# Loading the second piece of x over the scalar queue, ahead of the parameters

## The chip, the cores and the metric

The kernel runs on one core of one Trainium2 chip. The metric is the device time of one execution in microseconds (us); lower is better. Loads are DMA transfers from HBM to SBUF, stores go the other way. HBM is the memory of the chip, SBUF that of the core, with 128 partitions. Two queues are used: the sync queue (q1 in the profile, issued by SP) and the scalar queue (q10, issued by ACT). Both are worked off by the same 16 DMA engines. ACT is the engine that runs the ACTIVATE instructions (func(x * scale + bias)); PE multiplies matrices, DVE and POOL do the small rest, and SP only issues transfers here. A q behind an engine's name (ACTq, SPq) marks what its issuing part does.

## The reference

Batch normalisation with fixed statistics, then ReLU, on 16.8 MB of float32:

```python
def reference(x, gamma, beta, running_mean, running_var, eps):   # x: 32 x 128 x 32 x 32
    normalized = (x - running_mean[None, :, None, None]) / np.sqrt(running_var[None, :, None, None] + eps)
    scaled = normalized * gamma[None, :, None, None] + beta[None, :, None, None]
    return np.maximum(scaled, 0)
```

Per channel this is relu(x * scale + bias), so the kernel reads 16.8 MB, does one ACTIVATE per 128 x 1024 elements, and writes 16.8 MB.

## The kernel before

x is seen as 2 halves (t) of 128 partitions with 16 rows of 1024 numbers each (4 KB a row). It is loaded in six pieces; I call them x0, x2, x4, x8 (rows 0 to 2, 2 to 4, 4 to 8, 8 to 16 of the first half) and y0, y8 (rows 0 to 8 and 8 to 16 of the second).

```python
PIECES = (((0, 2), (2, 4), (4, 8), (8, 16)), ((0, 8), (8, 16)))
STORE_CUTS = {(0, 1)}
...
for t in range(T):
    for a, b in PIECES[t]:
        xt = data.tile([P, b - a, HW], F32, name=f"x{t}_{a}")
        nc.sync.dma_start(out=xt, in_=xr[t, :, a:b, :])
        tiles.append((t, a, b, xt))
raw = params.tile([Q, 4, J], F32, name="raw")
for k, src in enumerate((running_var, gamma, running_mean, beta)):
    nc.scalar.dma_start(out=raw[:, k, :], in_=src.rearrange("(q j) -> q j", j=J))
# ... cut: a matmul spreads the parameters, then sqrt, reciprocal, three products -> scale_t, bias_t
for t, a, b, xt in tiles:
    first = a
    for j in range(a, b):
        nc.scalar.activation(out=xt[:, j - a, :], in_=xt[:, j - a, :], func=ACTF.Relu,
                             bias=bias_t[:, j : j + 1], scale=scale_t[:, j : j + 1])
        if j + 1 == b or (t, j + 1) in STORE_CUTS:
            nc.scalar.dma_start(out=outr[t, :, first : j + 1, :], in_=xt[:, first - a : j + 1 - a, :])
            first = j + 1
```

A piece of n rows is one contiguous run of n x 4 KB on each partition. In the packet records a piece is 128 packets, one for each partition, that is 8 for each of 16 DMA engines: of 8 KB for x0, of 32 KB for x8, and so on. The first store is cut in two with 4 KB packets, those of x2, x4 and x8 have 8, 16 and 32 KB.

Of the kernel before, what the change touches and what calls it, by code (L numbers as in the profile page):

```python
# [1 line left out]

# [4 lines left out]


F32 = mybir.dt.float32
ACTF = mybir.ActivationFunctionType  # L10



J = 16

PIECES = (((0, 2), (2, 4), (4, 8), (8, 16)), ((0, 8), (8, 16)))

STORE_CUTS = {(0, 1)}


@with_exitstack
def kernel(
    ctx: ExitStack,
    tc: tile.TileContext,
    x: bass.AP,
    gamma: bass.AP,
    beta: bass.AP,
    running_mean: bass.AP,
    running_var: bass.AP,
    eps: bass.AP,  # L30
    out: bass.AP,
):
    nc = tc.nc
    B, C, H, W = x.shape
    HW = H * W
    P = nc.NUM_PARTITIONS
    assert C % J == 0 and P % (C // J) == 0 and (B * C) % (P * J) == 0
    Q = C // J
    T = B * C // (P * J)

    xr = x.rearrange("b c h w -> (b c) (h w)").rearrange("(t p j) w -> t p j w", p=P, j=J)
    outr = out.rearrange("b c h w -> (b c) (h w)").rearrange("(t p j) w -> t p j w", p=P, j=J)

    data = ctx.enter_context(tc.tile_pool(name="data", bufs=1))
    params = ctx.enter_context(tc.tile_pool(name="params", bufs=1))
    psum = ctx.enter_context(tc.tile_pool(name="psum", bufs=1, space=bass.MemoryType.PSUM))

    tiles = []
    for t in range(T):
        for a, b in PIECES[t]:  # L50
            xt = data.tile([P, b - a, HW], F32, name=f"x{t}_{a}")
            nc.sync.dma_start(out=xt, in_=xr[t, :, a:b, :])  # L52
            tiles.append((t, a, b, xt))


# [4 lines that stand above are left out]
    eps_t = params.tile([P, 1], F32, name="eps_t")  # L60
    nc.vector.memset(eps_t, float(eps))  # L61
    rep = params.tile([Q, P // Q, Q], F32, name="rep")
    nc.gpsimd.memset(rep, 1.0)  # L63
    nc.gpsimd.affine_select(  # L64
        out=rep,
        in_=rep,
        compare_op=mybir.AluOpType.is_equal,
        fill=0.0,
        base=0,
        pattern=[[0, P // Q], [-1, Q]],  # L70
        channel_multiplier=1,
    )
    cols = psum.tile([P, 4, J], F32, name="cols")
    nc.tensor.matmul(  # L74
        cols.rearrange("p k j -> p (k j)"),
        rep.rearrange("q r s -> q (r s)"),
        raw.rearrange("q k j -> q (k j)"),
        start=True,
        stop=True,
    )  # L80
    std_t = params.tile([P, J], F32, name="std_t")
    nc.scalar.activation(out=std_t, in_=cols[:, 0, :], func=ACTF.Sqrt, bias=eps_t[:, 0:1], scale=1.0)  # L82
    rstd_t = params.tile([P, J], F32, name="rstd_t")
    nc.vector.reciprocal(out=rstd_t, in_=std_t)  # L84
    scale_t = params.tile([P, J], F32, name="scale_t")
    nc.vector.tensor_mul(out=scale_t, in0=cols[:, 1, :], in1=rstd_t)  # L86
    ms_t = params.tile([P, J], F32, name="ms_t")
    nc.vector.tensor_mul(out=ms_t, in0=cols[:, 2, :], in1=scale_t)  # L88
    bias_t = params.tile([P, J], F32, name="bias_t")
    nc.vector.tensor_sub(out=bias_t, in0=cols[:, 3, :], in1=ms_t)  # L90

    with tc.manual_schedule(engines={mybir.EngineType.Activation}):
# [3 lines that stand above are left out]
                nc.scalar.activation(  # L96
                    out=xt[:, j - a, :],
                    in_=xt[:, j - a, :],
                    func=ACTF.Relu,
                    bias=bias_t[:, j : j + 1],  # L100
                    scale=scale_t[:, j : j + 1],
                )
                if j + 1 == b or (t, j + 1) in STORE_CUTS:
                    nc.scalar.dma_start(
                        out=outr[t, :, first : j + 1, :], in_=xt[:, first - a : j + 1 - a, :]
                    )
                    first = j + 1


# [1 line left out]
_INS = ['x', 'gamma', 'beta', 'running_mean', 'running_var', 'eps']  # L111
_OUTS = [((32, 128, 32, 32), 'float32')]

_NUMBERS = {'eps': 1e-05}


# [26 lines left out]
```

## Time and profile before

| | before |
|---|---|
| time, median of 3 runs | 83.86 us (83.7 to 83.93) |
| span in the profile | 81.9 us |
| packet time, both queues (96.2% of the span) | 78.8 us |
| ACT busy | 38.5 us |
| first ACTIVATE on x | 9.72 us |
| loads end, last store ends | 46.1 us, 80.6 us |

A queue row of the profile gives packets, megabytes, and the time of these packets as a share of 16 engines' span. Share times span is the time for which the average engine worked for this queue. A row of the windows gives from:to and length, busy time of PE, PEld, DVE, ACT and POOL, the clock of TensorE, the DMA share and GB/s. A packet counts where it starts, so a short window can show a share over 1.

### The profile page before, as it was taken

How to read it: one execution, taken by the hardware profiler on the slowest of the kernel's cores; microseconds unless marked ns; L12 is line 12 of the kernel's file. 1: busy time of each engine (PE TensorE's matmuls, PEld its weight loads, DVE VectorE, ACT ScalarE, POOL GpSimd, SP SyncE). 2: the span in 40 equal slices, each digit the busy share in tenths (PEclk: the TensorE clock that was granted, in tenths of full speed). 3: DMA queues.
4: the chain of work that ended last, by engine and by line, in shares of the span. 5: the costliest groups of instructions: out<-in, count | busy, mean ns of one | idle time of the engine just before them, and what ended most of it. 6: DMA issues, size and time to landing. Idle time of an engine off the chain costs nothing.

```text
span 81.9 us, 119 instructions
## 1 busy us (share of the span) xinstructions
PE 0.7 (1%) x2; PEld 0.5 (1%) x2; DVE 0.8 (1%) x5; ACT 38.5 (47%) x34; POOL 0.8 (1%) x6
## 2 busy tenths in 40 slices
PE   0002000000000000000000000000000000000000
PEld 0002000000000000000000000000000000000000
DVE  0000300000000000000000000000000000000000
ACT  0600377799039999199994199993000000000000
POOL 3000000000000000000000000000000000000000
DMA  2899999989899999979789798996999899799690
GB/s 32 328 425 472 408 448 448 512 352 494 370 448 416 446 418 396 500 296 600 320 380 580 304 464 384 512 512 288 480 512 400 368 512 448 320 512 496 272 512 0
DMA packets 1936, 33.56 MB, mean 410 GB/s; under 512 B 272, under 2 KB 272, under 8 KB 528
## 3 DMA queue, kind: packets, MB, share of 16 engines
q1 hardware_dynamic: 864, 16.78, 48.4%
q10 hardware_dynamic: 1072, 16.78, 47.8%
HBM read 16.78 MB, written 16.78 MB: 410 GB/s over the span
## 4 chain that ended last, share of the span: by engine, by line
DMA 56%; ACT 11%; SPq 0%; issue 0%
DMA x<-in_x_dram 56%; ACT x L96 11%; SPq L52 0%
## 5 line engine op out<-in xcount | busy, mean ns | idle before, releaser
L96 ACT ACTIVATE x<-x,bias_t,scale_t 128x1024 f32<-128x1024 f32 x32 | 37.0, 1228 | 10.3 <-DMA x<-in_x_dram 7.9
L82 ACT ACT_TABLE_LOAD x1 | 1.3, 1283 | 2.6 <-issue 2.6
L82 ACT ACTIVATE std_t<-cols,eps_t 128x16 f32<-128x16 f32 x1 | 0.3, 273 | 4.5 <-PE cols L74 4.5
L74 PE MATMUL cols<-raw,rep 8*128 8x64 f32 x2 | 0.7, 428 | 7.7 <-DMA raw<-in_beta_dram 7.7
L74 PEld LDWEIGHTS cols<-raw,rep 8*128 8x128 f32 x2 | 0.5, 304 | 7.7 <-issue 7.7
L64 POOL TENSOR_SCALAR_AFFINE_SELECT rep<-rep 8x128 f32<-8x128 f32 x1 | 0.4, 392 | 0.1
L84 DVE RECIPROCAL rstd_t<-std_t 128x16 f32<-128x16 f32 x1 | 0.3, 254 | 7.8 <-ACT std_t L82 7.8
L63 POOL MEMSET rep<- 8x128 f32 x1 | 0.2, 195 | 0.3 <-POOLq L124 0.3
L86 DVE TENSOR_TENSOR scale_t<-cols,rstd_t 128x16 f32<-128x16 f32 x1 | 0.2, 175 | 0.1
L90 DVE TENSOR_TENSOR bias_t<-cols,ms_t 128x16 f32<-128x16 f32 x1 | 0.2, 175 | 0.0
L88 DVE TENSOR_TENSOR ms_t<-cols,scale_t 128x16 f32<-128x16 f32 x1 | 0.2, 175 | 0.0
L124 POOL MEMSET const-bfloat16-1.0<- 128x1 bf16 x1 | 0.1, 106 | 0.0
L124 POOL MEMSET const-uint8-127<- 128x1 uint8 x1 | 0.1, 106 | 0.0
L124 POOL MEMSET const-float32-0.0<- 128x1 f32 x1 | 0.1, 103 | 0.3 <-issue 0.3
L124 POOL MEMSET const-float32-1.0<- 128x1 f32 x1 | 0.1, 103 | 0.0
L61 DVE MEMSET eps_t<- 128x1 f32 x1 | 0.1, 59 | 0.9 <-PEq L124 0.9
## 6 DMA issues: line engine op xcount, KB each, us to landing
x<-in_x_dram SPq DMA_DIRECT2D x3, 4096.0 KB, 38.8
out_dram<-x ACTq DMA_DIRECT2D x3, 4096.0 KB, 27.9
x<-in_x_dram SPq DMA_DIRECT2D x2, 1024.0 KB, 5.7
x<-in_x_dram SPq DMA_DIRECT2D x1, 2048.0 KB, 11.2
out_dram<-x ACTq DMA_DIRECT2D x1, 2048.0 KB
out_dram<-x ACTq DMA_DIRECT2D x2, 512.0 KB, 18.8
out_dram<-x ACTq DMA_DIRECT2D x1, 1024.0 KB
raw<-in_running_var_dram ACTq DMA_DIRECT2D x1, 0.5 KB
```

The source lines that it names most:

```text
L61: nc.vector.memset(eps_t, float(eps))
L63: nc.gpsimd.memset(rep, 1.0)
L64: nc.gpsimd.affine_select(out=rep, in_=rep, compare_op=mybir.AluOpType.is_equal, fill=0.0, base=0, pattern=[[0, P // Q], [-1, Q]], channel ...
L74: nc.tensor.matmul(cols.rearrange("p k j -> p (k j)"), rep.rearrange("q r s -> q (r s)"), raw.rearrange("q k j -> q (k j)"), start=True, s ...
L82: nc.scalar.activation(out=std_t, in_=cols[:, 0, :], func=ACTF.Sqrt, bias=eps_t[:, 0:1], scale=1.0)
L84: nc.vector.reciprocal(out=rstd_t, in_=std_t)
L86: nc.vector.tensor_mul(out=scale_t, in0=cols[:, 1, :], in1=rstd_t)
L88: nc.vector.tensor_mul(out=ms_t, in0=cols[:, 2, :], in1=scale_t)
L90: nc.vector.tensor_sub(out=bias_t, in0=cols[:, 3, :], in1=ms_t)
L96: nc.scalar.activation(out=xt[:, j - a, :], in_=xt[:, j - a, :], func=ACTF.Relu, bias=bias_t[:, j : j + 1], scale=scale_t[:, j : j + 1],)
L124: nc = _bacc.Bacc("TRN2", target_bir_lowering=False, num_devices=1)
```

## The change

The second piece, x2, is issued by ACT and not by SP, in front of the parameters. The intent is to have two pieces under way at once from the start.

```diff
+PIECES_SCALAR = (0, 2)
 ...
-            nc.sync.dma_start(out=xt, in_=xr[t, :, a:b, :])
+            eng = nc.scalar if (t, a) == PIECES_SCALAR else nc.sync
+            eng.dma_start(out=xt, in_=xr[t, :, a:b, :])
```

## The prediction

> **What bounds the kernel now.** I read the page first, then the chain of waits, the waits themselves, the windows and the timeline. The page's strip of DMA business and its queue rows:
>
> ```profile
> DMA  2899999989899999979789798996999899799690
> ...
> q1 hardware_dynamic: 864, 16.78, 48.4%
> q10 hardware_dynamic: 1072, 16.78, 47.8%
> HBM read 16.78 MB, written 16.78 MB: 410 GB/s over the span
> ```
>
> q1 is the sync queue (864 packets, all loads of x), q10 the scalar queue (four parameters and all stores). 48.4 + 47.8 = 96.2% of the span of 81.9 us, that is 78.8 us, is time in which the DMA engines work on a packet. That leaves 3.1 us. The windows say where it lies and how fast the rest runs (last columns: TensorE clock, DMA share, GB/s):
>
> ```profile
> 0.00:1.50 1.50, 0.00 (x0) 0.00 (x0) 0.06 (x1) 0.00 (x0) 0.80 (x6) 1.00 0.00 0
> 1.50:2.50 1.00, 0.00 (x0) 0.00 (x0) 0.00 (x0) 0.00 (x0) 0.00 (x0) 1.00 0.70 123
> 3.00:8.00 5.00, 0.27 (x2) 0.30 (x2) 0.00 (x0) 0.90 (x1) 0.00 (x0) 1.00 1.02 430
> 20.00:46.00 26.00, 0.00 (x0) 0.00 (x0) 0.00 (x0) 18.85 (x17) 0.00 (x0) 1.00 1.00 428
> 46.00:80.00 34.00, 0.00 (x0) 0.00 (x0) 0.00 (x0) 9.16 (x8) 0.00 (x0) 1.00 1.01 436
> 80.00:81.90 1.90, 0.00 (x0) 0.00 (x0) 0.00 (x0) 0.00 (x0) 0.00 (x0) 1.00 0.00 0
> ```
>
> There are 1.5 us before the first byte, about 1.5 us after the last one, and between them no hole: 430 GB/s with loads alone, 428 with loads and stores mixed, 436 with stores alone. So this is a copy of 33.56 MB at one rate. The chain names the load of x (56%) and the last eight ACTIVATEs (11%), and stops at 55.95 us:
>
> ```profile
> 7.99 38.77 DMA x<-in_x_dram
> 46.76 0.03 issue
> 46.79 9.16 ACT x L96 x8
> ```
>
> The chain follows waits between instructions, and nothing after 55.95 us waits except the program's end. The last store is issued at 55.97 us. The stores then take until 80.3 us, so at 434 GB/s 24.3 us x 434 = 10.5 MB were still to be written. The last store is 4.2 MB, that is 9.7 us. It could have come as late as 80.3 - 9.7 = 70.6 us without leaving the DMA engines a gap. **ACT has about 14.6 us of slack at the end**, and its idle time does not set the span.
>
> **What the Trainium skill says.** (1) "DMA: Bandwidth & Descriptors", section "Issuing engines are not separate DMA queues": transfers from sync and scalar run on the same 16 engines and interleave, and issuing from two engines saves only sequencer time. The trace agrees: the two queues together give 428 GB/s, one alone 430. (2) The same page, "Where 436 GB/s comes from", gives a ceiling of 435.2 GB/s; 428 to 436 here is that ceiling. (3) The same page, "Queues, rings and completion order": each DMA engine takes turns between the queues it has work for, packet by packet. The trace agrees in kind: in the mixed stage one load packet of 32 KB (1.213 us in the packet records) alternates with one store packet (0.159 us for 4 KB). (4) The same page, "Latency and other measured facts", gives about 600 ns to a first byte on these queues; here the first issue starts at 0.81 us and the first packet at about 1.5, so 0.7 us.
>
> **The change, part by part.**
>
> Removed from sync: the second issue (x rows 2 to 4, 1 MB). The issue took about 0.43 us, from 1.23 to 1.66 us. The issues of x4 and x8 move up by about that. Worth nothing by itself: the first piece keeps the engines in work for 1 MB / 430 GB/s = 2.4 us from 1.57 us on, and the second was in the queue by then.
>
> Added to scalar: the same issue in front of the four parameter issues, which begin now at 0.81 us:
>
> ```profile
> 0.81 7.51 SPq L52 DMA_DIRECT2D x<-in_x_dram  x6
> 0.81 0.59 ACTq L59 DMA_DIRECT2D raw<-in_running_var_dram  x1
> 1.43 0.29 ACTq L59 DMA_DIRECT2D raw<-in_gamma_dram  x1
> 1.75 0.31 ACTq L59 DMA_DIRECT2D raw<-in_running_mean_dram  x1
> 2.08 0.45 ACTq L59 DMA_DIRECT2D raw<-in_beta_dram  x1
> 7.73 0.65 PE L74 MATMUL cols<-raw,rep 8*128 8x64 f32 x2 [7.73 <-DMA raw<-in_beta_dram]
> ...
> 9.72 1.24 ACT L96 ACTIVATE x<-x,bias_t,scale_t 128x1024 f32<-128x1024 f32 x1 [1.03 <-DVE bias_t L90]
> ```
>
> The issues of the parameters start some 0.4 to 0.6 us later. The possible gain is in the ramp: from 1.5 to 2.5 us only 123 GB/s move, (430 - 123) / 430 = 0.7 us of lost transfer. The first packet of each engine takes up to 1.0 us where the later ones of 8 KB take 0.309. Two queues that open at once may cover part of that first wait. I allow **0 to 0.3 us, 0.1 expected**.
>
> The cost is in the order of the packets. Each engine holds 8 packets of x0 and 8 of x2. Before they came one after the other on one queue, x0 first. Now they take turns, so both end near 1.57 + 0.5 (first packet) + 16 x 0.309 = 7.0 us, landing at about 7.3 us. x0 landed at about 5.2 us before; x2 hardly moves. The parameters now stand behind x2 in the scalar queue. In the packet records of before, the later three went between load packets of 8 KB, data and completion write each taking a turn (0.31 us apart). After the change they meet the 16 KB packets of x4 (0.611 us): four data packets and four completion writes are eight turns, so about 7.0 + 7 x 0.61 = 11.3 us, with landing and semaphore 11.8 to 12.3 us, against 7.7 before. From the matmul to the first ACTIVATE it is 9.72 - 7.73 = 2.0 us, so **the first ACTIVATE moves from 9.72 to about 14 us**, with the first store behind it.
>
> What this costs at the end: nothing, by the slack. While there are no stores the loads take the whole rate; there are 16.78 MB of them, enough for 39 us, and a store delayed by 4.5 us only gives its turn to a load. ACT catches up, because it waits now for x anyway:
>
> ```profile
> ACT x L96 <- DMA x<-in_x_dram: 7.9, 3, 3.3
> DVE rstd_t L84 <- ACT std_t L82: 7.8, 1, 7.8
> PE cols L74 <- DMA raw<-in_beta_dram: 7.7, 1, 7.7
> ```
>
> The first eight tiles with their four store issues take 20.9 - 9.7 = 11.2 us, from 14 to about 25.4 us, instead of a wait for x8 that ended at 23.86. So x8 is started some 1.5 us later, x0 of the second half under 1 us later, and the last eight when their load lands, 46 to 47 us, as now. The last store goes out at about 56 us and the writing is still backlogged.
>
> A smaller move: semaphores are dealt out anew. Sync's issue of the second half's first piece waited for a parameter before (4.1 us, until 6.98); after the change it waits for x4, due at about 12.5 us. By then x8 (4.2 MB, 9.7 us of work) is queued, so the load queue does not run dry. The first store now also waits for x2, long landed by then.
>
> Sum: 83.86 - 0.1 (ramp) + 0 (parameters, absorbed) = **83.75 us**.
>
> **The rivals.** *A: parameters are late and this reaches the end.* For it: they stand behind 1 MB and the first ACTIVATE could be 4 to 5 us later. Against it: 14.6 us of slack in the last store, and 39 us of loads to fill the time. If there were an idle hole of the whole delay it would give about 88 us; a partial one 84.5 to 86. *B: the early start pays fully.* If the 0.7 us of ramp vanished, about 83.1 us. Against it: one queue with 1 MB in it already had work for each engine at 1.57 us; it was latency, not lack of packets, that held the rate down. *C: parameters come through quickly all the same*, because the second queue gets its turns: then the first ACTIVATE stays at 9.7 to 10.5 us, and the time is 83.8 as well. The time does not tell C from my account, the timeline does. *D: opening two read streams disturbs the rate*: a per cent less over the first 7 us is 0.07 us, so this is nothing.
>
> **Range and chances.** The bytes, packet sizes and rate are the same, and the three runs before lie within 0.23 us. Below 83.3 the ramp would have to give back over 0.5 us; above 84.3 a hole of half a microsecond would have to open. Hence 83.3 to 84.3. Faster by over 2% means under 82.2, 1.7 us less, more than the whole ramp: 2%. Slower by over 2% means over 85.5, which needs rival A to eat all of the slack: 3%. Within 2%: 95%.
>
> **What would show it.** Right: the two queues' shares still add up to about 78.8 us; the windows stay at 425 to 440 GB/s from 3 to 80 us; PE waits for a parameter until about 12 us and the first ACTIVATE starts near 14; ACT's wait for x falls from 7.9 us to 1 to 4; the last store is issued at 55 to 58 us. Wrong in a step: first ACTIVATE under 11 us (the packet order is not as I say) or over 16; a window between 12 and 50 us at a DMA share under 0.9 (the loads or stores ran dry); the window 1.5 to 2.5 at 300 GB/s or more (rival B).

## The result, and the profile after

The changed kernel takes 84.56 us (median of 6, 84.4 to 84.68), the kernel before 83.88 us in the same rounds. The ratio is 1.0081 (95% interval 1.0066 to 1.0095). It is slower by 0.7 us, within 2%, and above the predicted range of 83.3 to 84.3.

The page of the changed kernel, its DMA strip and queue rows:

```profile
DMA  1899897996999897979799999988996997999690
...
q10 hardware_dynamic: 1216, 17.83, 50.4%
q1 hardware_dynamic: 720, 15.73, 45.8%
```

Queue q10 has 1.05 MB more, q1 as much less: that is x2. The two shares still add up to 96.2%, but of 82.7 us: 79.6 us of packet time where it had been 78.8 (79.5 and 78.8 where the packet records are summed; the shares are rounded). **The 0.7 to 0.8 us are in the packets themselves**; no hole opened. The windows of the changed kernel:

```profile
1.50:2.50 1.00, 0.00 (x0) 0.00 (x0) 0.00 (x0) 0.00 (x0) 0.00 (x0) 1.00 0.59 131
3.00:8.00 5.00, 0.00 (x0) 0.00 (x0) 0.00 (x0) 1.26 (x1) 0.00 (x0) 1.00 1.03 434
20.00:46.00 26.00, 0.00 (x0) 0.00 (x0) 0.00 (x0) 23.70 (x21) 0.00 (x0) 1.00 0.97 404
46.00:80.00 34.00, 0.00 (x0) 0.00 (x0) 0.00 (x0) 9.16 (x8) 0.00 (x0) 1.00 1.02 439
```

The ramp moves 131 GB/s (123 before), so it gained almost nothing. The stores at the end run at 439. Of these stages only 20 to 46 us lost: 404 GB/s where it was 428. (Before and after cut a few packets differently at the window's edges, so the difference is rougher than it looks; the packet sums below are not.)

The timeline of the changed kernel, in its first 27 us:

```profile
0.80 0.41 ACTq L56 DMA_DIRECT2D x<-in_x_dram  x1
...
2.57 0.32 ACTq L63 DMA_DIRECT2D raw<-in_beta_dram  x1
...
13.00 0.66 PE L78 MATMUL cols<-raw,rep 8*128 8x64 f32 x2 [13.00 <-DMA raw<-in_beta_dram]
...
15.00 1.24 ACT L100 ACTIVATE x<-x,bias_t,scale_t 128x1024 f32<-128x1024 f32 x1 [1.02 <-DVE bias_t L94]
16.27 0.38 ACTq L108 DMA_DIRECT2D out_dram<-x  x1
...
26.22 9.16 ACT L100 ACTIVATE x<-x,bias_t,scale_t 128x1024 f32<-128x1024 f32 x8 [0.42 <-ACT x L100]
```

The matmul waits for beta until 13.00 us (7.73 before), so the first ACTIVATE starts at 15.00 (9.72) and the first store is issued at 16.27 (10.99), 5.3 us later. ACT catches up, as its waits and the end of the chain show:

```profile
PE cols L78 <- DMA raw<-in_beta_dram: 13.0, 1, 13.0
...
ACT x L100 <- DMA x<-in_x_dram: 1.2, 1, 1.2
```

```profile
46.16 0.04 ACT x L100
46.20 1.10 issue
47.31 8.01 ACT x L100 x7
```

ACT waits 1.2 us for x instead of 7.9, and the last eight ACTIVATEs end at 55.32 us (55.95 before). ACT is not late at the end; the stores are simply written until 81.4 us instead of 80.6.

**Which packets are slow.** The DMA shares and rates above are sums of the trace's packet records, one line for each packet with its start, size and time. In these nearly every packet takes exactly what its size asks for: 0.159 us for 4 KB, 0.309 for 8 KB, 0.611 for 16 KB, 1.213 for 32 KB. I summed, over all packets, the time beyond that and divided by 16 engines:

| lost time, us per engine | before | after | after, second profile |
|---|---|---|---|
| first packets, to 6 us | 0.44 | 0.35 | 0.65 |
| 6 us to the last two load packets of each engine | 0.19 | 0.29 | 0.11 |
| the last two load packets of each engine | 0.00 | 0.73 | 0.64 |

The packets of 32 KB are all of x8, y0 and y8. "The last two load packets" are the last two of y8: the point where an engine runs out of loads and goes over to stores alone. In the changed kernel they start at 41.7 and 43.8 us and take 1.76 and 1.40 us, on average over the engines; before, they took 1.213 each. Below I call this the tail loss. The first row varies by 0.3 us between two profiles of one kernel, so nothing is built on it.

### The profile page after: what moved, and what is told of

Its sections match the earlier page's. It is cut to its first block, busy times and chain, and to the rows that moved or that the text cites. A ratio compares the mean times of both kernels' runs of the same rounds, so it can differ in the third digit from the quotient of the medians.

```text
span 82.7 us, 121 instructions
## 1 busy us (share of the span) xinstructions
PE 0.7 (1%) x2; PEld 0.5 (1%) x2; DVE 0.8 (1%) x5; ACT 38.5 (47%) x34; POOL 0.8 (1%) x6
## 4 chain that ended last, share of the span: by engine, by line
DMA 54%; ACT 10%; issue 2%; SPq 1%
DMA x<-in_x_dram 54%; ACT x L100 10%; SPq L56 1%
## 6 DMA issues: line engine op xcount, KB each, us to landing
out_dram<-x ACTq DMA_DIRECT2D x2, 512.0 KB, 19.7
```

## The experiments

**Is it the kernel, and is it the delay?** `after_again` is the changed kernel unaltered.

> The changed kernel once more, for a second profile. If the extra 0.7 us is a property of the kernel and not of one execution, the time is 84.4 to 84.7 us, and the slow load packets (32 KB ones over 1.3 us, 0.7 us of transfer in all) lie again near 41 to 44 us. If they are chance, the time is again near 84.5 but the slow packets lie elsewhere.

It took 84.58 us (ratio 1.0076, interval 1.0056 to 1.0096), and its second profile is in the table above: the same packets are slow. The loss belongs to the kernel.

`e1_delay` is the kernel before with idle work on ACT in front of the first ACTIVATE on x:

```diff
+        for width in [1024, 1024, 1024, 1024, 512]:
+            nc.scalar.activation(out=scratch[:, :width], in_=scratch[:, :width], func=ACTF.Relu,
+                                 bias=bias_t[:, 0:1], scale=scale_t[:, 0:1])
         for t, a, b, xt in tiles:
 ... (cut: the scratch tile)
```

> The kernel before, with 4.5 idle ACTIVATEs on a scratch tile ahead of the first one on x, so that the first store comes about 5.3 us later, as in the changed kernel, and nothing else moves. Theory 1 (the late parameters cost the time, through the later start of the stores beside the loads): 84.4 to 84.7 us. Theory 2 (the second piece on the scalar queue costs it, by its place beside the first piece or by the semaphores dealt out anew): 83.7 to 84.0 us, as before.

It took 84.40 us (1.0057; 1.0043 to 1.0070). Its page and its timeline:

```profile
span 82.6 us, 125 instructions
...
q1 hardware_dynamic: 864, 16.78, 48.8%
q10 hardware_dynamic: 1072, 16.78, 47.3%
```

```profile
15.39 1.22 ACT L106 ACTIVATE x<-x,bias_t,scale_t 128x1024 f32<-128x1024 f32 x1
16.65 0.38 ACTq L114 DMA_DIRECT2D out_dram<-x  x1
```

Here q1 holds the loads of x and nothing else, as in the kernel before. There the loads took 48.4% of 81.9 = 39.6 us; here 48.8% of 82.6 = 40.3. The stores took 39.1 in both. So a late first store alone, with x2 on sync and the parameters on time, makes the loads 0.7 us dearer and accounts for 0.5 of the 0.7 us of the change. Its tail loss is 0.61 us.

`e2_behind` puts x2 on the scalar queue behind the parameters.

```diff
-            nc.sync.dma_start(out=xt, in_=xr[t, :, a:b, :])
+            if (t, a) != (0, 2):
+                nc.sync.dma_start(out=xt, in_=xr[t, :, a:b, :])
 ... (after the four parameters)
+    nc.scalar.dma_start(out=tiles[1][3], in_=xr[0, :, 2:4, :])
```

> The second piece on the scalar queue, but issued behind the four parameters. The parameters land early, the sync queue's waits are those of the changed kernel. Theory 1 (late parameters): first ACTIVATE at 8 to 10 us and 83.7 to 84.0 us. Theory 2 (piece on the scalar queue, or the sync queue's later issue of the second half): 84.4 to 84.7 us.

It took 84.51 us (1.0075; 1.0061 to 1.0089), as theory 2 said. But it does not decide for it, because it brought a delay of its own: the first ACTIVATE came at 11.23 us, and then ACT stood idle for 6.0 us until x2 was there at 20.1. The first store was issued at 12.50 us, but it stood behind x2 in the scalar queue: its first packet came at 17.1 us (14.6 before, 19.7 in the changed kernel). The tail loss was 0.57 us. The run does not separate the theories.

`e3_store_sync` issues every store on sync, so that all stores stand behind all loads in one queue.

```diff
-                    nc.scalar.dma_start(
+                    nc.sync.dma_start(
                         out=outr[t, :, first : j + 1, :], in_=xt[:, first - a : j + 1 - a, :]
```

> The kernel before with all stores issued on sync, so that they stand behind all loads on one queue and no load packet runs beside a store. If load packets lose time only where stores mix with them, the loads end near 40.5 us, the sum of packet times falls by 0.2 us and the time is 83.5 to 83.8 us. If the slow packets come without stores too, 83.9 to 84.6 us.

It took 84.77 us (1.0104; 1.0086 to 1.0121). No store packet lies beside a load packet here, and all 32 KB load packets take 1.213 us until 38.7 us; then the last two of each engine lose 1.10 us. So the tail loss needs no store among the loads. My idea that mixing is what costs was wrong.

**Is it the place in the stream, or what stands behind it?** `e4_swap` is e3 with `((8, 16), (0, 8))` as the second half of PIECES, so y8 before y0.

> All stores on sync behind the loads, as in the third experiment, with the last two 4 MB loads in the other order. There the slow packets were the last two of each engine in the last load, 1.1 us in all. If it is the place in the stream (the end of the loads, before the stores begin), they are again the last two of the last load, at 38 to 41 us, and the time is again about 84.8 us. If it is the address in x, they move with the piece to 28 to 31 us.

84.70 us (1.0109; 1.0090 to 1.0127), and again the last two packets of the last load lose 1.04 us. It is the place, not the address. `e5_apart` is e3 with ACT held until the last load has landed (cut: the scratch tile):

```diff
+        nc.scalar.copy(out=scratch, in_=tiles[-1][3][:, 7, 0:1])
         for t, a, b, xt in tiles:
```

> The same with ACT held until the last load has landed, so that no store is in any queue while loads run; the DMA engines stand idle for some 2 to 3 us between, so the time is 86 to 88 us whatever the theory. If the last load packets are slow because stores come behind them in the queue, all load packets of 32 KB now take 1.21 us. If the reads themselves are slow there, the last two of the last load are slow again, by about 1.1 us in all.

93.75 us, far more than the 86 to 88 that I had written: without any store in the queue ACT becomes the bound of the second half (35 us of ACTIVATEs in a row). For the question this does not matter. With no store behind the loads, the last two load packets lose 0.01 us. So **the last load packets are slow only when stores stand behind them**. `e13_few_behind`, run later, gives a dose: the same, but half of the first row, 16 KB for each DMA engine, is stored early and stands behind the loads (the diff is cut to this store).

```diff
+        nc.scalar.activation(out=x0[0:64, 0, :], in_=x0[0:64, 0, :], func=ACTF.Relu,
+                             bias=bias_t[0:64, 0:1], scale=scale_t[0:64, 0:1])
+        nc.sync.dma_start(out=outr[0, 0:64, 0:1, :], in_=x0[0:64, 0:1, :])
         nc.scalar.copy(out=scratch, in_=tiles[-1][3][:, 7, 0:1])
```

> ACT and the stores held until the last load has landed, but with 16 KB of store data for each DMA engine (four packets of 4 KB) standing behind the loads on the sync queue. With nothing behind them the last load packets lost nothing, with all stores behind them 1.1 us (4 KB packets) or 1.6 us (32 KB packets). If what is lost is the time in which store data is fetched ahead while the last load packets are written, at most 16 KB at 27 B/ns, 0.6 us, is lost now, and about 0.4 to 0.6 us is expected. If any store behind the loads costs the whole, 1.1 us. The total is about 94 us in either case.

94.25 us in all, and a tail loss of 0.40 us. None behind gives 0.01, 16 KB gives 0.40, all of them 1.10. ACT was idle from 10.98 to 42.41 us in e13, so the loss does not need ACT at work beside the loads, which e5 had taken away together with the stores.

**What of the stores matters?** `e6_delay2` is e1 with two idle ACTIVATEs of 1024 columns.

> The kernel before with two idle ACTIVATEs, a delay of 2.4 us instead of 5.8. Each load packet gives one turn to a store packet, so the first two stores (4 KB packets) last some 18 turns and the third (8 KB packets) then begins about two load packets later than before, still beside the last two load packets. If 8 KB store packets beside the last load packets are what hides their slowness, the time is 83.8 to 84.0 us. If the loss grows with the delay as such, 84.1 to 84.3 us.

84.36 us (1.0063; 1.0046 to 1.0080), tail loss 0.51 us. There were 8 KB store packets beside the last load packets, and they did not help: my theory that they hide the loss fell. Nor does the loss grow in proportion to the delay, since 2.4 us cost nearly as much as 5.7. `e7_uncut` is the changed kernel with `STORE_CUTS = set()`.

> The changed kernel with the first store not cut in two, so that its packets are 8 KB, as are those of the second store; both then last until the loads end, and the last load packets have 8 KB store packets beside them although the stores start late. If those hide the slowness, the time falls from 84.55 to 83.8 to 84.0 us. If the late start as such costs it, 84.4 to 84.7 us.

84.15 us (1.0036; 1.0023 to 1.0049), between the two ranges. The profile says why: the tail loss is gone (0.01 us) although the first store is issued at 17.68 us, but 0.48 us are lost in the last two packets of x8, at 19 to 22 us, just where the first stores enter.

Next I thought that small store packets behind the last load were at fault. Three kernels tested it. `e8_big_first` keeps all stores on sync and sends the 32 KB packets of x8 first (cut: the old issue that this replaces):

```diff
+                    held.append((outr[t, :, first : j + 1, :], xt[:, first - a : j + 1 - a, :]))
                     first = j + 1
+            if t > 0 or a == 8:
+                for dst, src in held[::-1]:
+                    nc.sync.dma_start(out=dst, in_=src)
+                held = []
```

> All stores on sync behind the loads, but the store with 32 KB packets goes first and those with 16, 8 and 4 KB packets follow. Theory 3 (the last load packets of an engine are held up when small store packets stand directly behind them; large ones do not do it): the last two packets of the last load take 1.21 us each, and the time falls from 84.77 to 83.6 to 83.8 us. Theory 4 (any change from loads alone to stores alone costs about 1.1 us): 84.6 to 84.8 us.

85.00 us (1.0126; 1.0111 to 1.0141), tail loss 1.58 us: with large packets behind the loads the loss was greater than with small ones. Theory 3 was refuted. `e9_order` is the changed kernel with the store of x2 issued behind that of x4:

```diff
+                    if (t, a) == (0, 2):
+                        held = dst, src
+                        continue
+                    nc.scalar.dma_start(out=dst, in_=src)
+                    if (t, a) == (0, 4):
+                        nc.scalar.dma_start(out=held[0], in_=held[1])
```

> The changed kernel with two stores issued in the other order: that of x4 (16 KB packets) ahead of that of x2 (8 KB). The stores start as late as in the changed kernel. Theory 3: 16 KB packets now stand behind the last load packets, the 0.6 to 0.7 us at 41 to 44 us are gone, the 0.1 to 0.25 us at 19 to 21 us stay: 83.9 to 84.15 us. If the late start as such costs the time: 84.4 to 84.7 us.

84.21 us (1.0035; 1.0022 to 1.0047), a little above the range; but the reason given was wrong, since 0.44 us of tail loss stayed. `e10_cut` is the kernel before with `STORE_CUTS = {(0, 1), (0, 6)}`: x4 is stored in two parts with 8 KB packets.

> The kernel before with the store of x4 cut in two, so that its packets are 8 KB instead of 16. Nothing starts later, nothing changes queues; only the packets behind the last load packets are smaller. Theory 3: the last load packets lose 0.4 to 0.8 us and the time rises from 83.85 to 84.2 to 84.7 us. If the late start as such is what costs time in the changed kernel: 83.8 to 84.0 us.

83.84 us (0.9995; 0.9980 to 1.0011) and no tail loss. Theory 3 had asked for a loss here too.

The next guess was that a store's end marker (its completion write) near the end of the loads stops whatever happens. `e11_split32` and `e12_split64` are the changed kernel with the store of x2 cut by partitions:

```diff
+                    cuts = (0, 32, P) if (t, a) == (0, 2) else (0, P)      # e12: 64
+                    for p, r in zip(cuts, cuts[1:]):
+                        nc.scalar.dma_start(out=outr[t, p:r, first : j + 1, :],
+                                            in_=xt[p:r, first - a : j + 1 - a, :])
```

> The changed kernel with the store of x2 cut by partitions, 32 and 96, so that a store's end marker (completion write) comes two 8 KB packets after the last 4 KB one, beside the last load packet, about where it lies in the kernel before. Bytes, packet sizes and the late start stay. Theory 5 (the last load packets are held up by store data fetched ahead into the pipeline behind them, and a store's end marker close to the end of the loads stops that fetching): the 0.6 to 0.7 us at 41 to 44 us go down below 0.2, the time is 83.9 to 84.1 us. Theory 6 (the loss goes with the late start, by something that no store boundary touches): 84.4 to 84.7 us.

> The same with the cut at 64 partitions: the end marker comes four 8 KB packets after the last 4 KB one, two packets behind the last load packet, as in the run with a delay of 2.4 us, which lost 0.5 us there. Theory 5: 0.3 to 0.6 us lost at 41 to 44 us, 84.2 to 84.5 us. Theory 6: 84.4 to 84.7 us, as with 32 partitions.

84.48 us (1.0068; 1.0052 to 1.0084) and 84.77 us (1.0104; 1.0085 to 1.0122), with tail losses of 0.54 and 0.44 us. The marker did its move and the loss stayed: theory 5 was refuted. (Why e12 is 0.3 us above e11 with the same packet sums was not followed up.) `e14_delay1` is e1 with one idle ACTIVATE.

> The kernel before with one idle ACTIVATE, 1.2 us of delay. The 4 KB stores then end about one load packet later than before. Theory 5: the end marker of the third store lies one or two packets behind the last load packet, so 0 to 0.3 us lost there, 83.8 to 84.2 us. Theory 6, loss growing with the delay: between 83.85 and 84.36 us as well, 84.0 to 84.2. The place and size of the slow packets in its profile is what counts.

83.96 us (1.0013; 0.9998 to 1.0028), tail loss 0.09 us: between a delay of 1.2 us and one of 2.4 the tail loss jumps from 0.09 to 0.51.

**A rule that was tried before it was believed.** With these profiles side by side one number orders the kernels that store beside their loads: how many KB of stores each engine had written when its loads ended (all store packets that had ended at the median end of the engines' last load packets, over 16). It led to the last three runs. `e15_cut2` is the kernel before with `STORE_CUTS = {(0, 1), (0, 3)}`: x2 too is stored in 4 KB packets. Nothing starts later.

> The kernel before with the store of x2 cut in two as well, so that its packets are 4 KB: nothing starts later, no queue changes, but fewer store bytes are written beside the loads (one store packet goes with each load packet). In the profiles so far the tail loss is 0 where 112 KB per DMA engine or more had been stored when the loads ended, 0.09 us at 104, 0.5 at 96, 0.45 to 0.73 at 72 to 80. Here about 85 KB. Theory 7 (what counts is how many store bytes got out beside the loads, however that comes about): 0.4 to 0.7 us lost in the last two load packets, 84.2 to 84.6 us. Theory 6 (the late start as such): no loss, 83.8 to 84.0 us.

84.50 us (1.0072; 1.0056 to 1.0088), tail loss 0.68 us at 88 KB. Its page, and beneath it that of e10, which has one cut more than before in another place:

```profile
span 82.8 us, 121 instructions
...
q1 hardware_dynamic: 864, 16.78, 48.7%
```

```profile
span 82.1 us, 121 instructions
...
q1 hardware_dynamic: 864, 16.78, 48.5%
```

The loads of e15 took 48.7% of 82.8 = 40.3 us, those of e10 48.5% of 82.1 = 39.8, those of the kernel before 39.6. In e15 no store was late and no transfer changed queue, and the loss is as in the changed kernel. **So the late start as such is not needed: a finer cut of the stores, with which fewer store bytes get out beside the loads, is enough.** `e16_before_uncut` is the kernel before with `STORE_CUTS = set()`.

> The kernel before with the first store not cut: the first store starts some 2.5 us later (first and second row together) but with 8 KB packets, so that about 170 KB per engine are stored when the loads end. Theory 7: no loss in the last load packets; 0.1 to 0.5 us may be lost where the stores begin; 83.7 to 84.2 us. Theory 6: a loss of 0.3 to 0.5 us at 42 to 46 us, 84.2 to 84.4 us.

84.19 us (1.0038; 1.0017 to 1.0058): by the time alone either theory could claim it, but there is no tail loss, with 208 KB stored, though its first store is issued 1.05 us later than before (12.04 us). It loses 0.79 us elsewhere: 0.26 at 13 to 16 us, where the stores begin, and the rest scattered up to 43 us. `e17_params_pool` is the changed kernel with the parameters on the gpsimd queue.

```diff
-        nc.scalar.dma_start(out=raw[:, k, :], in_=src.rearrange("(q j) -> q j", j=J))
+        nc.gpsimd.dma_start(out=raw[:, k, :], in_=src.rearrange("(q j) -> q j", j=J))
```

> The changed kernel with the four parameters loaded over the gpsimd queue, so that they do not stand behind the second piece. If the second queue costs nothing by itself and only the late parameters did: first ACTIVATE at 8 to 10.5 us, 112 KB or more stored per engine when the loads end, no loss in the last load packets, 83.6 to 84.0 us. If the second piece on the scalar queue has a cost of its own: 84.2 to 84.6 us with an early first ACTIVATE.

84.40 us (1.0056; 1.0039 to 1.0073). The parameters were not early, as the timeline shows:

```profile
3.02 0.52 POOL L63 DMA_DIRECT2D raw<-in_beta_dram  x1
...
10.16 0.65 PE L78 MATMUL cols<-raw,rep 8*128 8x64 f32 x2 [10.16 <-DMA raw<-in_beta_dram]
```

Beta was issued by 3.54 us and the matmul still waited for it until 10.16. The first ACTIVATE came at 12.14 us (I had written 8 to 10.5), 96 KB were stored by the end of the loads, and the tail loss was 0.28 us. This fits the order of the table below. But the tail loss is only half of the 0.53 us by which the run is slower than the kernel before, so it does not exclude a small cost of the second queue.

All kernels whose stores run beside the loads, by that number:

| kernel | KB stored per engine when the loads end | tail loss, us | lost elsewhere after 6 us, us | median, us |
|---|---|---|---|---|
| e2 x2 behind parameters | 84 (about 72 on 8 engines, 96 on 8) | 0.57 | 0.33 | 84.51 |
| e1 delay 5.7 us | 72 | 0.61 | 0.29 | 84.40 |
| e11 / e12 marker moved | 72 / 72 | 0.54 / 0.44 | 0.18 / 0.31 | 84.48 / 84.77 |
| after, two profiles | 72 / 72 | 0.73 / 0.64 | 0.29 / 0.11 | 84.56 / 84.58 |
| e9 x4 ahead of x2 | 80 | 0.44 | 0.30 | 84.21 |
| e15 4 KB for x2 too | 88 | 0.68 | 0.13 | 84.50 |
| e6 delay 2.4 us | 96 | 0.51 | 0.24 | 84.36 |
| e17 parameters on gpsimd | 96 | 0.28 | 0.33 | 84.40 |
| e14 delay 1.2 us | 104 | 0.09 | 0.53 | 83.96 |
| before | 112 | 0.00 | 0.19 | 83.88 |
| e10 8 KB for x4 | 112 | 0.00 | 0.36 | 83.84 |
| e7 after, uncut | 129 | 0.01 | 0.49 | 84.15 |
| e16 before, uncut | 208 | 0.00 | 0.79 | 84.19 |

Up to 96 KB there is a tail loss of 0.28 to 0.73 us, at 104 KB it is 0.09, from 112 KB on it is nothing. The rule is empirical. It was formed on the rows without e15, e16 and e17; e15 and e16 came out in the tail as it said, on either side. The KB are not separated from a second number that orders these kernels about as well: how many load packets each engine still had after its last 4 KB store packet. That is about 8 in the kernel before and in e10, 7 in e14 (0.09 us), 6 in e6 and e17, 3 in the changed kernel and none in e15; e7 and e16 have no 4 KB store packets and no tail loss. No run changed one number and held the other. No version beats the kernel before: e10 is its equal.

## Why the prediction was wrong

- **The bound** was right: a copy at one rate, with ACT off the path. The last store was issued at 55.35 us (55 to 58 predicted) and ACT's wait for x fell to 1.2 us (1 to 4).
- **The ramp** was right in kind: 0 to 0.3 us were allowed and 0.1 expected. The window 1.5 to 2.5 us moved 131 GB/s where it had been 123, worth 0.02 us. Rival B, the early start that pays, is out.
- **The order of the packets** was right and a little short: the matmul was to have its parameters at 11.8 to 12.3 us and had them at 13.00; the first ACTIVATE was to start near 14 us and started at 15.00. In the packet records x0 and x2 end at 7.2 to 7.6 us (7.0 predicted) and the last end marker of a parameter comes at 12.4 (11.3). Rival C is out.
- **ACT's recovery** was mis-sized without consequence: x8 was to start 1.5 us later and started 26.22 - 23.86 = 2.4 us later, y0 1.0 us later, y8 0.6 us earlier.
- **The semaphores** did as told: sync's issue of the second half's first piece waited for x4 until 13.10 us (12.5 predicted), and the load queue did not run dry.
- **Small misreadings** did no harm. The packet times of the prediction are about 0.3 us early against the profile's: the first load packet starts at 1.84 us and not at 1.57, the last store ends at 80.6 and not 80.3, so ACT's slack was 14.9 us. From the first issue at 0.81 us to the first load packet it is 1.03 us, not 0.7; the 600 ns of the page fit only if counted from the end of that issue at 1.18 us (0.66). And 14 + 11.2 is 25.2, not 25.4.
- **The step that failed** is "What this costs at the end: nothing, by the slack", with its ground, "a store delayed by 4.5 us only gives its turn to a load", and the sum's term "+ 0 (parameters, absorbed)". It took every packet to cost the same wherever it lies. The slack in ACT was real, but it says only that no hole opens. The check that I had named first, shares that still add up to 78.8 us, came out at 79.6. Trading turns between loads and stores was not free: with 72 KB of stores per engine beside the loads instead of 112, the last two load packets of each engine took 0.64 to 0.73 us longer in sum. e1 shows that the delay alone does it (0.5 of the 0.7 us), e15 that the same loss comes without any delay when the stores are cut finer and fewer of their bytes go beside the loads.
- **Rival A** had the size (84.5 to 86 for a partial effect) but not the mechanism: it spoke of an idle hole, and the DMA engines were never idle. Rival D, a disturbed rate in the first 7 us, is out too: 434 GB/s from 3 to 8 us.

**What stays open.** Why the last load packets are held up. Shown is that it needs stores behind the loads (e3 against e5), that it grew with how much stood behind in three runs (0.01, 0.40, 1.10 us), that it follows the place and not the address (e4), and that it is neither due to small packets behind them (e8, e10) nor prevented by a store's end marker (e11). One account would fit e3, e5, e8 and e13: an engine fetches store data ahead while it still writes its last loads, and the two get in each other's way. The 0.40 us of e13 are less than the 0.6 us that 16 KB take at the 27 KB per us of a 32 KB packet, which this account allows. One more thing in the records fits: with loads in the queues the first store packet came 3.65 us after the start of its issue (10.99 to 14.64 us, the kernel before), in e5 with nothing else to move 0.85 us (43.52 to 44.37). The difference is 2.3 load packets of 1.213 us, as if about two stood already taken in; no run tested that. The account does not say why 112 KB of stores beside the loads make the tail loss vanish, so I do not call it the cause. Also open is whether the second queue has a cost of its own: e1 without it is 0.16 us below the changed kernel, with intervals that overlap.

## What to carry to other kernels

Slack on the compute engine shows that a delay opens no hole; it does not show that the transfers cost the same in another order. In a kernel bound by DMA, multiply the queues' shares by the span before and after: if the product grew, the packets themselves got slower, and the packet records show which. Don't put a small transfer that everything waits for behind a large one in the same queue: here four loads of 0.5 KB behind 1 MB released the matmul at 13.00 us instead of 7.73, and at 9.24 when they stood ahead of it (e2).

## What the Trainium skill lacked or had wrong

- "DMA: Bandwidth & Descriptors", section "Issuing engines are not separate DMA queues", says that issuing from several engines only saves issue time. It does not say what a small transfer then waits for. The order can be worked out from the page's section on queues, as the prediction did, but no number is given: four loads of 0.5 KB behind 1 MB in the scalar queue released the matmul at 13.00 us instead of 7.73, and on the gpsimd queue, issued by 3.54 us, at 10.16.
- The same page, section "Queues, rings and completion order", gives about 9 to 17 descriptors as the typical packet that is drained in one turn. In the mixed stage here a turn was one partition's run of a piece: one record of 32 KB (1.213 us) against one of 4 KB (0.159 us) or 8 KB (0.309 us).
- The same page, section "Where 436 GB/s comes from", gives the 435.2 GB/s that the prediction used, but also says that for HBM to SBUF and back the HBM side binds at about 358. Here, with one core at work, it did not: 430 GB/s with loads alone, 436 with stores alone.
- No page that I found says that load packets slow down where an engine passes from loads to stores: 1.10 us per engine with all stores behind the loads in 4 KB packets first, 1.58 us with 32 KB packets first, 0.01 us with none behind. The large-packet order, which I expected to be harmless, was the worst.
- None has the dependence on the stores written beside the loads: 0.28 to 0.73 us lost up to 96 KB per engine, none from 112 KB on.
